# Product-key experts: 52 activation rows and 32 gate rows kept, one-hots by pairs of tokens, another spill layout

## The chip, the cores and the metric

The kernel runs on one core of one Trainium2 chip. The metric is the device time of one launch in microseconds. The core has TensorE (PE in the rows; PEld is its weight load), VectorE (DVE), ScalarE (ACT), GpSimd (POOL) and SyncE (SP, which here only issues DMAs), and 16 DMA engines.

## The reference, cut to what matters

The network has two blocks over 256 tokens of width 1024 (272 with the meta tokens in the first). The change lies in the last layer, a product-key mixture of 128 x 128 single-neuron experts:

```
q = (tok @ w_q)                                  # 8 heads x 2 halves x 128
s = einsum('nhpc,hpkc->nhpk', q, sub_keys)       # 128 scores per half
s_top, i_top = top_k(s, 16)                      # 16 keys of each half
best, pos = top_k(s_top[0] + s_top[1], 16)       # 16 pairs per head: 128 experts a token
gate = softmax(best)
act = gelu(u_emb[expert] . tok) * gate
out = sum over the 128 experts of act * v_emb[expert]
```

The kernel does not gather rows of u_emb and v_emb. It computes gelu(u . tok) for all 16384 experts, multiplies by a dense gate that is zero outside the selected experts, and multiplies by all of v_emb.

## The kernel before, in words

All matrix products are split into a high and a low part (three fp32r products each: L311, L312, L313). A weight tile of 128x1024 comes by DMA into `st` (3 buffers), ScalarE writes its high half `wh` (L279), VectorE or GpSimd the low half `wl` (L280; `lo_engine` says which); `wh` and `wl` have 5 buffers each. Weights are taken in a fixed order: 16 tiles of `wq`, then the `pu` tiles (rows of u_emb, one tile of 128 experts for each value of the first key), then `pv` tiles (v_emb).

An expert block k is a pair: `ublock(k)` (24 products of 128x256 into `pu`, then gelu) and `vblock(k)` (12 products of 128x512 into four accumulators `peo`). Between them `gated` multiplies by the gate row k and splits (`bh`, `bl`).

The layer has a front and a tail. In the front the first N1 = 39 ublocks are computed and their activations kept in `H`, while the experts are being selected: `top16` and `select` work on VectorE (L1538 to L1591), then `gates()` builds the dense gate. For 4 tokens at a time `onehot` makes `gO` (one-hot of both keys, [128, 2, 128, 4], tokens innermost; L1703) and `gW` (the first one-hot times the high and the low part of the gate; L1705), both fp16; `product` multiplies the second key's one-hot (stationary) with the two weighted ones, 2 products of 128x128 per token (`pG`, L1715 and L1716), and ScalarE puts columns 0 to 38 into `G1` (kept, L1718) and the other 89 into a staging tile `gst` of 32 tokens (L1719), which goes out to `peGd` in device memory in four DMAs (L1741). How much of this stands between two ublocks is set by a budget: each ublock adds GB = 3.0 (GB2 = 5.0 in the gate stage), each step of the generator takes off a figure that stands for its time:

```
due += self.GB2 if self.grp else self.GB
while gen is not None and due > 0:
    step = next(gen, None)
    ...
```

The list scheduler of the framework then orders the instructions of each engine by its own costs; each engine issues its own list strictly in order.

Behind the front, 39 vblocks use `H` and `G1`; then in the tail ublock(k + 1) and vblock(k) alternate for the other 89, with gate rows read back from `peGd` two at a time (`gl`, L1808). In the front the low halves of `wq` and `pu` are made by GpSimd, all later ones by VectorE.

Of the kernel before, what the change touches and what calls it, by code (L numbers as in the profile page):

```python
# [21 lines left out]
P = 128  # L22
# [15 lines left out]
# ---------------------------------------------------------------- host layout  # L38
# [17 lines left out]
def prep(i):  # L56
# [34 lines left out]
    # second block  # L91
# [32 lines left out]
def shape_consts():  # L124
    """Masks and selectors that depend on shapes alone."""
    a = {}
    p = np.arange(P)
    hd, ix = p // 64, p % 64
    same = hd[:, None] == hd[None, :]
    m = np.arange(64)[None, :]  # L130
    lt = (ix[:, None] < m).astype(np.float32)
    a["k_mask"] = np.ascontiguousarray(np.stack([lt, ix[:, None] <= m, -lt], axis=1).astype(np.float32))
    t, u = ix[:, None], ix[None, :]
    lv = []
    for b in (16, 32):
# [21 lines left out]
class Null:  # L157
    """Takes any call; used to walk the program once for the order in which it uses its weights."""
# [20 lines left out]
# ---------------------------------------------------------------- kernel  # L179
class Kern:  # L180
# [50 lines left out]
    # ---- weight stream  # L231
# [17 lines left out]
    def lo_engine(self, key, k):  # L249
        if key[0] == "wq" or (key[0] == "pu" and key[1] < self.N1):  # L250
            return self.nc.gpsimd
        if key[0] in ("w_rw", "w_ml", "w_gt") and k % self.PM == 0:
            return self.nc.gpsimd
        return self.nc.vector
# [60 lines left out]
    # ---- rms statistics  # L315
# [64 lines left out]
    def post(self, fg, ssq, h, T, name):  # L380
        """h += fg * rstd; returns the per-chunk updater."""
# [11 lines left out]
    # ---- FFN  # L393
# [55 lines left out]
    # ---- neighbourhood attention  # L449
# [13 lines left out]
    def na(self, xh, xl, R, gpost):  # L463
# [12 lines left out]
        nc.gpsimd.dma_start(bq, io["na_bqkv"])  # L476
        nc.vector.tensor_scalar_mul(bq[:, 0:8], bq[:, 0:8], 0.125)
        bo = ap.tile([P, C], F32, name="na_bo")
        nc.gpsimd.dma_start(bo, io["na_bo"])
# [199 lines left out]
    # ---- differential attention  # L679
    def da(self, xh, xl, R, gpost):  # L680
# [12 lines left out]
        nc.gpsimd.dma_start(sg, io["da_sg"])  # L693
        nc.vector.tensor_scalar_mul(sg, sg, 1.0 - LAMBDA_INIT)
        lp = ap.tile([P, 4, 64], F32, name="da_lp")
        nc.gpsimd.dma_start(lp.rearrange("p a b -> p (a b)"), io["da_lam"].to_broadcast([P, 256]))
# [187 lines left out]
    # ---- second block: mixers  # L884
# [10 lines left out]
    def mixers(self, h, xh, xl, R):  # L895
# [103 lines left out]
        def head_in(hh, S):  # L999
            """projections of a head: q, k with their convolution, v, output gate"""  # L1000
# [31 lines left out]
        def head_mid(hh, S):  # L1032
            """scores, their product with the values, mean and variance"""
# [48 lines left out]
        def heads_out():  # L1082
            """norm of all heads and output gate"""
# [23 lines left out]
        def filler():  # L1107
            """half a projection at a time, each followed by a step of what is due"""
# [36 lines left out]
        # ------------------------------------------------ RWKV  # L1145
# [129 lines left out]
        # [chunk, c, row, column] of 128 x 128 with 128 words between: diagonal blocks lie at one stride  # L1275
# [49 lines left out]
        def solve():  # L1325
            """inverse of the 128 unit triangular 16 x 16 blocks on the diagonals"""
# [145 lines left out]
        # ------------------------------------------------ merge, output  # L1472
# [52 lines left out]
    # ---- product-key experts  # L1525
    N1 = 39
# [4 lines left out]
    GB2 = 5.0  # L1531
# [12 lines left out]
    def select(self, tp, scr, b, v, ix, out):  # L1544
        """from the best 16 keys of each half to the 128 experts of a token; yields the time of each step"""
# [48 lines left out]
    def peer(self, h):  # L1594
        nc, io = self.nc, self.io
        T, N1 = NT, self.N1
        N2 = P - N1
# [9 lines left out]
        iota4 = ap.tile([P, P, 4], F16, name="iota4")  # L1607
        nc.vector.tensor_copy(iota4, self.iota.unsqueeze(2).to_broadcast([P, P, 4]))
# [30 lines left out]
        H = ap.tile([P, N1, T], F32, name="peH")  # L1639
        G1 = ap.tile([P, N1, T], F32, name="peG1")  # L1640
        gd = dp.tile([P, N2, T], F32, name="peGd")

        # ---- queries, scores, the best 16 keys of each half
# [25 lines left out]
        def gates():  # L1669
# [25 lines left out]
            # gate of every expert and token, G[i2, i1, t]  # L1695
            SG = self.SG
            sh = [P, 2, P, 4]
            gs_ = gst_.enter_context(self.tc.tile_pool(name="pegs", bufs=2))
            with self.tc.tile_pool(name="peg", bufs=2) as gp:
                def onehot(t1):  # L1700
                    tb = slice(t1, t1 + 4)
                    OB, W = (gp.tile(sh, F16, tag=f"g{n}", name=f"g{n}_{t1}") for n in "OW")
                    nc.vector.tensor_tensor(OB, iota4[:, None].to_broadcast(sh),  # L1703
                                            iT[:, :, None, tb].to_broadcast(sh), op=ALU.is_equal)
                    nc.vector.tensor_mul(W, OB[:, 0:1].to_broadcast(sh), gT[:, :, None, tb].to_broadcast(sh))  # L1705
                    return t1, OB, W

                def product(t1, OB, W):
# [4 lines left out]
                    p = self.acc(f"pG_{t1}").rearrange("p (t e) -> p t e", t=4)  # L1713
# [3 lines left out]
                    pe = p.rearrange("p t e -> p e t")  # L1717
                    nc.scalar.mul(G1[:, :, t1:t1 + 4], pe[:, 0:N1], 1.0 / self.GS)  # L1718
                    nc.scalar.mul(st[:, :, t1 - t0:t1 - t0 + 4], pe[:, N1:], 1.0 / self.GS)  # L1719
                    if t1 + 4 == t0 + SG:  # L1720
                        spills.extend((t0, st, slice(N2 * q // 4, N2 * (q + 1) // 4)) for q in range(4))
                    if t1 // 4 % 2:
                        spill()
# [3 lines left out]
                for t1 in range(0, T, 4):  # L1727
                    wait.append(onehot(t1))
                    if len(wait) > 1:
                        product(*wait.pop(0))  # L1730
                    yield 1.3
# [20 lines left out]
        for k in range(N1):  # L1752
# [28 lines left out]
        def gated(k, a, g):  # L1781
            ah = a2.tile([P, T], F32R, tag="bh", name=f"bh_{k}", bufs=3)
            al = a2.tile([P, T], F32R, tag="bl", name=f"bl_{k}", bufs=3)
            i = nc.vector.tensor_mul(a, a, g)
            j, _ = self.split(a, ah, al)
            if k < N1:
# [7 lines left out]
        for k in range(N1):  # L1794
# [8 lines left out]

        def ub(k):
            if (k - N1) % 2 == 0:
                n = min(2, P - k)
                g = vp.tile([P, 2, T], F32, tag="gl", name=f"gl_{k}", bufs=3)
                nc.sync.dma_start(g[:, :n], gd[:, k - N1:k - N1 + n])  # L1808
                hb["g"] = g
            a = vp.tile([P, T], F32, tag="ha", name=f"ha_{k}")  # L1810
            ublock(k, a)
            hb[k] = gated(k, a, hb["g"][:, (k - N1) % 2])

        fg = H[:, 0:4].rearrange("p k t -> p (k t)")
        ub(N1)
        for k in range(N1, P - self.FIN):
            if k == N1 + 8:
# [31 lines left out]
    # ---- whole  # L1849
# [54 lines left out]
```

## Time and profile before

| what | value |
|---|---|
| median of 3 runs | 2359.03 us (2357.69 to 2366.51) |
| span of the profiled execution | 2363.3 us; the page gives no other time of it, so the span stands for its time |
| TensorE busy in it | 2258.3 us, 96% |
| mean granted clock | 0.976 |
| front: first ublock to first output product | 1528.5 to 1746.2 us |
| 39 vblocks from kept rows | 1746.2 to about 1856 us |
| tail, 89 pairs | about 1856 us to the end |

A busy TensorE is not a TensorE at its peak, since its products are pipelined: how far apart two products start says more than how long one lasts. "issue" in a view is time in which an engine waited for nothing that the profile shows.

### The profile page before, as it was taken

The numbers are of one execution on the slowest core, as the hardware profiler recorded it, in microseconds if no ns is written. First come the engines' busy times: TensorE is split into PE (matmuls) and PEld (weight loads), VectorE is DVE, ScalarE is ACT, GpSimd is POOL, SyncE is SP. The second block draws the span as 40 slices with busy tenths as digits, with TensorE's granted clock in tenths as the row PEclk, the third lists the DMA queues.
The fourth block names the chain that finished last, engine by engine and source line by source line (L and its number), as shares of the span: only waits on it lengthen the run. The fifth ranks groups of instructions, "written<-read, shape, count | busy, mean of one in ns | idle before, by whom it ended". The sixth has DMA issues, their size and how long they took to land. (4 is left out here: it accounts for less than half of the span.)

```text
span 2363.3 us, 42332 instructions
## 1 busy us (share of the span) xinstructions
PE 2258.3 (96%) x16616; PEld 2148.1 (91%) x16616; DVE 1570.7 (66%) x2834; ACT 1170.8 (50%) x1992; POOL 380.8 (16%) x335
## 2 busy tenths in 40 slices
PE   8999999999999999999878999987999999999998
PEld 8999989999999889999878998986888899999997
DVE  6656777664765677765689647897777555555555
ACT  6444655443544456554544544544455444444444
POOL 1101211110210121210361112773200000000000
PEclk9999999999999999999989999997999999999999
DMA  6555433555455443555434325444896566666664
GB/s 207 178 169 160 149 109 115 183 170 176 153 178 173 140 142 102 182 183 182 141 105 126 119 68 184 161 152 97 144 203 227 200 210 209 210 214 209 210 209 144
DMA packets 217143, 389.56 MB, mean 165 GB/s; under 512 B 110272, under 2 KB 120272, under 8 KB 216816
## 3 DMA queue, kind: packets, MB, share of 16 engines
q1 hardware_dynamic: 216800, 386.71, 53.1%
q8 instruction: 131, 2.15, 0.4%
q14 instruction: 68, 0.56, 0.1%
q0 software_dynamic: 144, 0.15, 0.0%
HBM read 371.87 MB, written 14.94 MB: 164 GB/s over the span
## 5 line engine op out<-in xcount | busy, mean ns | idle before, releaser
L279 ACT ACTIVATE wh<-st 128x1024 fp32r<-128x1024 f32 (+2 forms) x680 | 703.8, 1037 | 789.1 <-PE peo L1773 146.9
L280 DVE TENSOR_TENSOR wl<-st,wh 128x1024 fp32r<-128x1024 f32 (+2 forms) x610 | 750.4, 1231 | 488.2 <-ACT wh L279 486.4
L311 PE MATMUL pg_ffn<-xh_n,wh 128*128 128x272 f32 (+1 forms) x1408 | 406.6, 291 | 12.7 <-ACT wh L279 8.1
L313 PE MATMUL pg_ffn<-xh_n,wl 128*128 128x272 f32 (+1 forms) x1408 | 408.1, 291 | 0.4 <-DVE wl L280 0.4
L312 PE MATMUL pg_ffn<-xl_n,wh 128*128 128x272 f32 (+1 forms) x1408 | 407.7, 290 | 0.0
L311 PE MATMUL pu<-xh_pe,wh 128*128 128x256 f32 x1024 | 292.5, 286 | 0.8 <-ACT peH L1748 0.8
L313 PE MATMUL pu<-xh_pe,wl 128*128 128x256 f32 x1024 | 291.2, 284 | 0.0
L312 PE MATMUL pu<-xl_pe,wh 128*128 128x256 f32 x1024 | 291.1, 284 | 0.0
L311 PEld LDWEIGHTS pg_ffn<-xh_n,wh 128*128 128x128 f32 x1408 | 268.4, 192 | 13.1 <-ACT wh L279 8.1
L313 PEld LDWEIGHTS pg_ffn<-xh_n,wl 128*128 128x128 f32 x1408 | 269.6, 192 | 0.8 <-DVE wl L280 0.8
L312 PEld LDWEIGHTS pg_ffn<-xl_n,wh 128*128 128x128 f32 x1408 | 270.1, 192 | 0.1
L280 POOL TENSOR_TENSOR wl<-st,wh 128x1024 fp32r<-128x1024 f32 x70 | 172.1, 2471 | 257.4 <-ACT wh L279 236.5
L1773 PE MATMUL peo<-wh,bh 128*128 128x512 f32 x512 | 203.0, 399 | 1.1 <-ACT bh L459 1.1
L1773 PE MATMUL peo<-wh,bl 128*128 128x512 f32 x512 | 202.1, 395 | 0.0
L311 PE MATMUL pd_ffn<-mh_ffn,wh 128*128 128x272 f32 (+1 forms) x704 | 201.9, 287 | 0.0
L1773 PE MATMUL peo<-wl,bh 128*128 128x512 f32 x512 | 201.4, 393 | 0.0
L312 PE MATMUL pd_ffn<-ml_ffn,wh 128*128 128x272 f32 (+1 forms) x704 | 201.4, 286 | 0.0
L313 PE MATMUL pd_ffn<-mh_ffn,wl 128*128 128x272 f32 (+1 forms) x704 | 201.3, 286 | 0.0
L311 PEld LDWEIGHTS pu<-xh_pe,wh 128*128 128x128 f32 x1024 | 196.1, 192 | 5.1 <-ACT peH L1748 1.0
L312 PEld LDWEIGHTS pu<-xl_pe,wh 128*128 128x128 f32 x1024 | 196.7, 192 | 3.6
L313 PEld LDWEIGHTS pu<-xh_pe,wl 128*128 128x128 f32 x1024 | 196.7, 192 | 0.1
L409 POOL TENSOR_TENSOR t_ffn<-t_ffn,t_ffn 128x272 f32<-128x272 f32 (+1 forms) x88 | 73.6, 838 | 455.3 <-DVE t_ffn L408 390.4
(626 smaller groups left out, 4747.4 us busy)
## 6 DMA issues: line engine op xcount, KB each, us to landing
st<-wgu SPq DMA_DIRECT2D x176, 512.0 KB, 3.5
st<-pu SPq DMA_DIRECT2D x128, 512.0 KB, 3.3
st<-pv SPq DMA_DIRECT2D x128, 512.0 KB, 3.4
st<-wd SPq DMA_DIRECT2D x64, 448.0 KB, 3.3
st<-wd SPq DMA_DIRECT2D x32, 512.0 KB, 3.4
st<-na_qkv SPq DMA_DIRECT2D x24, 512.0 KB, 3.4
st<-da_qkv SPq DMA_DIRECT2D x24, 512.0 KB, 3.7
gl<-peGd SPq DMA_DIRECT2D x44, 256.0 KB, 3.7
```

Source lines behind the costliest of these rows:

```text
L279: i1 = nc.scalar.activation(hi[:, :w], s[:, :w], AF.Copy)
L280: i2 = self.lo_engine(plan[k], k).tensor_sub(lo[:, :w], s[:, :w], hi[:, :w].bitcast(F32))
L311: mm(out, wh, xh, start=start, stop=False, **kw)
L312: mm(out, wh, xl, start=False, stop=False, **kw)
L313: mm(out, wl, xh, start=False, stop=stop, **kw)
L409: nc.gpsimd.tensor_mul(t2[:, :T], t1[:, :T], t2[:, :T])
L1773: mm(po[2 * b + j], x_[:, b * P:(b + 1) * P], w_[:, 4 * j:4 * j + 4].rearrange("p k m -> p (k m)"), start=k == 0 and n == 0, stop=k == P - ...
```

## The change

1. `H` keeps 52 rows in place of 39 (NH), `G1` keeps 32 in place of 39 (NG); gate rows 32 to 127 (96 in place of 89) go through device memory. So 13 ublocks move from the tail into the front, and vblocks 32 to 51 read their gate rows back.
2. One step of the gate stage is 8 tokens in place of 4: four VectorE instructions of 128x1024 (O1, W0, W1, O2), each of shape [4, 128, 2], two tokens innermost. TensorE reads the one-hots at a step of 2 fp16 elements in place of 4. O1 has one buffer, the others two.
3. The budget is taken off after each of the four instructions (0.7), and GB2 is 2.1.
4. `peGd` is laid out by blocks of 32 tokens, so that a spill writes runs of 3 KB per partition in place of 128 bytes, and a read-back reads runs of 256 bytes in place of 2 KB.
5. GpSimd makes the low halves of `pu` only up to k = 30 (NP); VectorE makes them from 31 on.
6. Four small loads of the attention stages go from GpSimd's queue to SyncE's, and the scratch of the software DMA queue is cut to 2048 bytes.

```diff
-        if key[0] == "wq" or (key[0] == "pu" and key[1] < self.N1):
+        if key[0] == "wq" or (key[0] == "pu" and key[1] < self.NP):
...
-        nc.gpsimd.dma_start(bq, io["na_bqkv"])
+        nc.sync.dma_start(bq, io["na_bqkv"])
...
-    N1 = 39
+    NH = 52
+    NG = 32
+    NP = 31
...
-    GB2 = 5.0
+    GB2 = 2.1
...
-        H = ap.tile([P, N1, T], F32, name="peH")
-        G1 = ap.tile([P, N1, T], F32, name="peG1")
-        gd = dp.tile([P, N2, T], F32, name="peGd")
+        H = ap.tile([P, NH, T], F32, name="peH")
+        G1 = ap.tile([P, NG, T], F32, name="peG1")
+        gd = dp.tile([T // SG, P, N2, SG], F32, name="peGd")
...
-                def onehot(t1):
-                    tb = slice(t1, t1 + 4)
-                    OB, W = (gp.tile(sh, F16, tag=f"g{n}", name=f"g{n}_{t1}") for n in "OW")
-                    nc.vector.tensor_tensor(OB, iota4[:, None].to_broadcast(sh),
-                                            iT[:, :, None, tb].to_broadcast(sh), op=ALU.is_equal)
-                    nc.vector.tensor_mul(W, OB[:, 0:1].to_broadcast(sh), gT[:, :, None, tb].to_broadcast(sh))
-                    return t1, OB, W
+                def pairs(x, t1):
+                    return x[:, t1:t1 + 8].rearrange("p (q s) -> p q s", s=2).unsqueeze(2).to_broadcast(sh)
+                def onehot(t1):
+                    O1, O2, W0, W1 = (gp.tile(sh, F16, tag=f"g{n}", name=f"g{n}_{t1}", bufs=1 if n == "O1" else 2)
+                                      for n in ("O1", "O2", "W0", "W1"))
+                    nc.vector.tensor_tensor(O1, iota2[:, None].to_broadcast(sh), pairs(iT[:, 0], t1), op=ALU.is_equal)
+                    yield 0.7
+                    nc.vector.tensor_mul(W0, O1, pairs(gT[:, 0], t1))
+                    yield 0.7
+                    nc.vector.tensor_mul(W1, O1, pairs(gT[:, 1], t1))
+                    yield 0.7
+                    nc.vector.tensor_tensor(O2, iota2[:, None].to_broadcast(sh), pairs(iT[:, 1], t1), op=ALU.is_equal)
+                    wait.append((t1, O2, W0, W1))
+                    yield 0.7
...
-                    for q in range(4):
-                        mm(p[:, q], OB[:, 1, :, q], W[:, 0, :, q], start=True, stop=False)
-                        mm(p[:, q], OB[:, 1, :, q], W[:, 1, :, q], start=False, stop=True)
+                    for u in range(0, 8, 4):
+                        p = self.acc(f"pG_{t1}_{u}").rearrange("p (t e) -> p t e", t=4)
+                        for q in range(4):
+                            a, b = divmod(u + q, 2)
+                            mm(p[:, q], O2[:, a, :, b], W0[:, a, :, b], start=True, stop=False)
+                            mm(p[:, q], O2[:, a, :, b], W1[:, a, :, b], start=False, stop=True)
...
-                nc.sync.dma_start(gd[:, q, t0:t0 + self.SG], st[:, q])
+                nc.sync.dma_start(gd[t0, :, q], st[:, q])
...
-        for k in range(N1):
+        for k in range(NH):
             ublock(k, H[:, k])
...
-        for k in range(N1):
+        for k in range(NG):
             vblock(k, *gated(k, H[:, k], G1[:, k]))
...
+        def spilled(k):
+            if (k - NG) % 2 == 0:
+                n = min(2, P - k)
+                g = vp.tile([P, T // SG, 2, SG], F32, tag="gl", name=f"gl_{k}", bufs=3)
+                nc.sync.dma_start(g[:, :, :n], gd[:, :, k - NG:k - NG + n].rearrange("u p k t -> p u k t"))
+                hb["g"] = g
+            return hb["g"][:, :, (k - NG) % 2]
...
+        for k in range(NG, NH):
+            vblock(k, *gated(k, H[:, k], spilled(k)))
...
-    nc = bacc.Bacc("TRN2", target_bir_lowering=False, num_devices=1)
+    nc = bacc.Bacc("TRN2", target_bir_lowering=False, num_devices=1, dynamic_dma_scratch_size=2048)
```

TensorE's list up to the gate stage is the same in both kernels. The next rows are TensorE's at the end of the front of the kernel before; `pu_20648` is the last of the 39 ublocks, each `pG` piece 8 products of 4 tokens, `peo` the first output products.

```order
L1716 MATMUL pG_20555<-gW_20536,gO_20535 128x128
L311 MATMUL pu_20603<-xh_pe,wh_20332 128x256
...
L311 MATMUL pu_20648<-xh_pe,wh_20410 128x256
...
L1715 MATMUL pG_20570<-gW_20552,gO_20551 128x128
...
L1715 MATMUL pG_20586<-gW_20567,gO_20566 128x128
...
L1715 MATMUL pG_20629<-gW_20583,gO_20582 128x128
...
L312 MATMUL pu_20648<-xl_pe,wh_20410 128x256
...
L1773 MATMUL peo_20674<-wh_20505,bh_20678 128x512
```

The same place in the changed kernel; `pu_20765` is the last of the 52 ublocks, and the number behind gW and gO is a step's first token.

```order
L311 MATMUL pu_20703<-xh_pe,wh_20539 128x256
...
L1728 MATMUL pG_0_20730<-gW_168_20596,gO_168_20595 128x128
...
L311 MATMUL pu_20765<-xh_pe,wh_20601 128x256
...
L1728 MATMUL pG_0_20793<-gW_176_20692,gO_176_20691 128x128
...
L1728 MATMUL pG_0_20824<-gW_184_20755,gO_184_20754 128x128
...
L1728 MATMUL pG_0_20856<-gW_192_20818,gO_192_20817 128x128
...
L1728 MATMUL pG_0_21066<-gW_248_21037,gO_248_21036 128x128
...
L1785 MATMUL peo_21090<-wh_20636,bh_21094 128x512
```

Before, the last gate products stand inside the last ublock. Now 22 of the 32 steps stand between ublocks 22 and 51 (three steps to four ublocks, each step's 16 products in one piece), and the steps of tokens 176 to 255, ten of them, stand behind the last ublock with nothing between them.

VectorE's list in the middle of the gate stage of the kernel before, with the low halves on GpSimd's own list:

```order
L1703 TENSOR_TENSOR gO_20362<-iota_17358,pei 128x1024
L1703 TENSOR_TENSOR gO_20377<-iota_17358,pei 128x1024
L1705 TENSOR_TENSOR gW_20363<-gO_20362,peg 128x1024
L1705 TENSOR_TENSOR gW_20378<-gO_20377,peg 128x1024
L1703 TENSOR_TENSOR gO_20393<-iota_17358,pei 128x1024
```

And of the changed kernel, where the low halves stand on VectorE's list from ublock 31 on:

```order
L280 TENSOR_TENSOR wl_20540<-st_20413,wh_20539 128x1024
L1711 TENSOR_TENSOR gW_152_20470<-gO_152_20468,peg 128x1024
L1713 TENSOR_TENSOR gW_152_20471<-gO_152_20468,peg 128x1024
L1715 TENSOR_TENSOR gO_152_20469<-iota_17358,pei 128x1024
L1709 TENSOR_TENSOR gO_160_20531<-iota_17358,pei 128x1024
L280 TENSOR_TENSOR wl_20602<-st_20475,wh_20601 128x1024
```

Per 8 tokens both lists hold four instructions of 128x1024; what is new on VectorE's list is the low halves between them.

## Rows read from the trace of the kernel before

**Rows 1.** Page: busy time of each engine; granted clock in 40 slices.

```profile
PE 2258.3 (96%) x16616; PEld 2148.1 (91%) x16616; DVE 1570.7 (66%) x2834; ACT 1170.8 (50%) x1992; POOL 380.8 (16%) x335
...
PEclk9999999999999999999989999997999999999999
```

**Rows 2.** Stretches from A to B: length, busy per engine, clock, DMA share, GB/s.

```profile
1530.00:1584.00 54.00, 53.23 (x446) 52.70 (x446) 53.44 (x164) 32.16 (x40) 47.10 (x20) 1.00 0.51 172
1584.00:1600.00 16.00, 4.50 (x36) 4.33 (x35) 15.03 (x32) 2.43 (x5) 0.15 (x1) 0.75 0.12 41
1600.00:1612.00 12.00, 5.17 (x36) 5.08 (x35) 12.00 (x12) 4.56 (x7) 9.87 (x4) 0.78 0.38 133
1612.00:1746.00 134.00, 118.96 (x938) 114.18 (x935) 102.78 (x129) 62.42 (x162) 33.65 (x13) 0.93 0.78 136
...
1860.00:2340.00 480.00, 480.00 (x3073) 433.53 (x3073) 266.91 (x343) 228.95 (x342) 0.00 (x0) 1.00 0.63 210
```

**Rows 3.** Waits, 1600 to 1746 us: waiting, waited for, total, times, longest.

```profile
DVE gO L1703 <- PE pG L1716: 30.4, 50, 2.4
PE pG L1715 <- DVE gW L1705: 21.0, 13, 6.8
```

**Rows 4.** Timeline of VectorE and GpSimd in the gate stage: start, length, instruction.

```profile
1608.72 2.84 DVE L1705 TENSOR_TENSOR gW<-gO,peg 128x1024 f16<-128x1024 f16 x1
...
1611.69 0.68 DVE L1705 TENSOR_TENSOR gW<-gO,peg 128x1024 f16<-128x1024 f16 x1
...
1653.49 2.39 POOL L280 TENSOR_TENSOR wl<-st,wh 128x1024 fp32r<-128x1024 f32 x1 [6.47 <-ACT wh L279]
1654.63 2.41 DVE L1703 TENSOR_TENSOR gO<-iota,pei 128x1024 f16<-128x1024 f16 x2 [1.80 <-PE pG L1716]
1656.96 1.28 DVE L1705 TENSOR_TENSOR gW<-gO,peg 128x1024 f16<-128x1024 f16 x2
```

**Rows 5.** Tile gO: ns min/median/max, first and last start.

```profile
L1716 PE MATMUL pG<-gW,gO x256: 293/298/303, 1611.7 to 1744.6; 128*128 128x128 f16 x128
L1703 DVE TENSOR_TENSOR gO<-iota,pei x64: 678/693/2851, 1600.6 to 1741.9; 128x1024 f16<-128x1024 f16 x64
L1705 DVE TENSOR_TENSOR gW<-gO,peg x64: 676/684/2842, 1608.7 to 1742.7; 128x1024 f16<-128x1024 f16 x64
```

**Rows 6.** Groups by line, 1612 to 1746 us: busy us, mean ns.

```profile
L280 DVE TENSOR_TENSOR wl<-st,wh 128x1024 fp32r<-128x1024 f32 x2 | 2.4, 1224 | 0.2 <-ACT wh L279 0.2
```

**Rows 7.** Timeline of TensorE, gate and block products: start, length.

```profile
1613.19 0.30 PE L1716 MATMUL pG<-gW,gO 128*128 128x128 f16 x1
...
1613.90 0.30 PE L1716 MATMUL pG<-gW,gO 128*128 128x128 f16 x1
...
1614.52 0.41 PE L311 MATMUL pu<-xh_pe,wh 128*128 128x256 f32 x1
1614.73 0.41 PE L312 MATMUL pu<-xl_pe,wh 128*128 128x256 f32 x1
...
1616.98 0.30 PE L1716 MATMUL pG<-gW,gO 128*128 128x128 f16 x1
...
1618.15 0.30 PE L1716 MATMUL pG<-gW,gO 128*128 128x128 f16 x1
```

**Rows 8.** Chain of waits: start, length; end of front, and two tail pairs.

```profile
1746.18 109.47 PE peo L1773 x468
...
1990.98 2.80 PE peo L1773 x12
...
1996.61 2.80 PE peo L1773 x12
```

**Rows 9.** DMA, 1620 to 1760 us: packets; queue's packets, MB, share of 16 engines.

```profile
DMA packets 88516, 20.76 MB, mean 148 GB/s; under 512 B 86144, under 2 KB 86144, under 8 KB 88504
...
q1 hardware_dynamic: 88504, 20.60, 82.7%
```

**Rows 10.** DMA, 1860 to 2300 us: the same.

```profile
DMA packets 28167, 92.63 MB, mean 211 GB/s; under 512 B 3136, under 2 KB 3136, under 8 KB 28135
...
q1 hardware_dynamic: 28135, 92.18, 62.9%
```

More of the change, by code (lines that the diff above doesn't have):

```diff
@@ L475, in na @@
         bq = ap.tile([P, 24], F32, name="na_bq")
-        nc.gpsimd.dma_start(bq, io["na_bqkv"])
+        nc.sync.dma_start(bq, io["na_bqkv"])
         nc.vector.tensor_scalar_mul(bq[:, 0:8], bq[:, 0:8], 0.125)
         bo = ap.tile([P, C], F32, name="na_bo")
-        nc.gpsimd.dma_start(bo, io["na_bo"])
+        nc.sync.dma_start(bo, io["na_bo"])
         vph, vpl, qms = [], [], []
@@ L692, in da @@
         sg = ap.tile([P, 1], F32, name="da_sg")
-        nc.gpsimd.dma_start(sg, io["da_sg"])
+        nc.sync.dma_start(sg, io["da_sg"])
         nc.vector.tensor_scalar_mul(sg, sg, 1.0 - LAMBDA_INIT)
         lp = ap.tile([P, 4, 64], F32, name="da_lp")
-        nc.gpsimd.dma_start(lp.rearrange("p a b -> p (a b)"), io["da_lam"].to_broadcast([P, 256]))
+        nc.sync.dma_start(lp.rearrange("p a b -> p (a b)"), io["da_lam"].to_broadcast([P, 256]))
         lt = ap.tile([P, 2, 64], F32, name="da_lt")
@@ L1595, in peer @@
         nc, io = self.nc, self.io
-        T, N1 = NT, self.N1
-        N2 = P - N1
+        T, NH, NG = NT, self.NH, self.NG
+        N2 = P - NG
         mm = nc.tensor.matmul
@@ L1606, in peer @@
         nc.vector.tensor_copy(self.iota16, self.iota[:, 0:16].unsqueeze(2).to_broadcast([P, 16, 16]))
-        iota4 = ap.tile([P, P, 4], F16, name="iota4")
-        nc.vector.tensor_copy(iota4, self.iota.unsqueeze(2).to_broadcast([P, P, 4]))
+        iota2 = ap.tile([P, P, 2], F16, name="iota2")
+        nc.vector.tensor_copy(iota2, self.iota.unsqueeze(2).to_broadcast([P, P, 2]))
         ssq = self.new_ssq("pe")
@@ L1638, in peer @@
         iT = ap.tile([P, 2, T], F16, name="pei")
-        H = ap.tile([P, N1, T], F32, name="peH")
-        G1 = ap.tile([P, N1, T], F32, name="peG1")
-        gd = dp.tile([P, N2, T], F32, name="peGd")
+        H = ap.tile([P, NH, T], F32, name="peH")
+        G1 = ap.tile([P, NG, T], F32, name="peG1")
+        SG = self.SG
+        gd = dp.tile([T // SG, P, N2, SG], F32, name="peGd")
         ts_ = ExitStack()
@@ L1694, in gates, with product @@
             ts_.close()
-            SG = self.SG
-            sh = [P, 2, P, 4]
+            sh = [P, 4, P, 2]
             gs_ = gst_.enter_context(self.tc.tile_pool(name="pegs", bufs=2))
             with self.tc.tile_pool(name="peg", bufs=2) as gp:
+                def pairs(x, t1):
+                    return x[:, t1:t1 + 8].rearrange("p (q s) -> p q s", s=2).unsqueeze(2).to_broadcast(sh)
                 def onehot(t1):
-                    tb = slice(t1, t1 + 4)
-                    OB, W = (gp.tile(sh, F16, tag=f"g{n}", name=f"g{n}_{t1}") for n in "OW")
-                    nc.vector.tensor_tensor(OB, iota4[:, None].to_broadcast(sh),
-                                            iT[:, :, None, tb].to_broadcast(sh), op=ALU.is_equal)
-                    nc.vector.tensor_mul(W, OB[:, 0:1].to_broadcast(sh), gT[:, :, None, tb].to_broadcast(sh))
-                    return t1, OB, W
-                def product(t1, OB, W):
+                    O1, O2, W0, W1 = (gp.tile(sh, F16, tag=f"g{n}", name=f"g{n}_{t1}", bufs=1 if n == "O1" else 2)
[9 more added lines that the diff above has]
+                    yield 0.7
+                def product(t1, O2, W0, W1):
                     nonlocal st
@@ L1712, in product @@
                         st = gs_.tile([P, N2, SG], F32, tag="gst", name=f"gst_{t1}")
-                    p = self.acc(f"pG_{t1}").rearrange("p (t e) -> p t e", t=4)
-                    for q in range(4):
-                        mm(p[:, q], OB[:, 1, :, q], W[:, 0, :, q], start=True, stop=False)
-                        mm(p[:, q], OB[:, 1, :, q], W[:, 1, :, q], start=False, stop=True)
[L1717 to L1723, printed above, removed]
+                    for u in range(0, 8, 4):
[4 more added lines that the diff above has]
+                            mm(p[:, q], O2[:, a, :, b], W1[:, a, :, b], start=False, stop=True)
+                        pe = p.rearrange("p t e -> p e t")
+                        t2 = t1 + u
+                        nc.scalar.mul(G1[:, :, t2:t2 + 4], pe[:, 0:NG], 1.0 / self.GS)
+                        nc.scalar.mul(st[:, :, t2 - t0:t2 - t0 + 4], pe[:, NG:], 1.0 / self.GS)
+                    if t1 + 8 == t0 + SG:
+                        spills.extend((t0 // SG, st, slice(N2 * q // 4, N2 * (q + 1) // 4)) for q in range(4))
+                    spill()
                 st, wait = None, []
                 self.grp = True
-                for t1 in range(0, T, 4):
-                    wait.append(onehot(t1))
+                for t1 in range(0, T, 8):
+                    yield from onehot(t1)
                     if len(wait) > 1:
                         product(*wait.pop(0))
-                    yield 1.3
                 for x in wait:
@@ L1783, in gated @@
             al = a2.tile([P, T], F32R, tag="bl", name=f"bl_{k}", bufs=3)
-            i = nc.vector.tensor_mul(a, a, g)
+            if k < NG:
+                i = nc.vector.tensor_mul(a, a, g)
+            else:
+                a3 = a.rearrange("p (u t) -> p u t", t=SG)
+                i = nc.vector.tensor_mul(a3, a3, g)
             j, _ = self.split(a, ah, al)
-            if k < N1:
+            if k < NH:
                 for n in range(self.AH):
@@ L1802, in peer @@
         vp = vs.enter_context(self.tc.tile_pool(name="pev", bufs=2))
-        def ub(k):
[L1805 to L1809, printed above, removed]
+        def spilled(k):
[5 more added lines that the diff above has]
+            return hb["g"][:, :, (k - NG) % 2]
+        def ub(k):
+            g = spilled(k)
             a = vp.tile([P, T], F32, tag="ha", name=f"ha_{k}")
             ublock(k, a)
-            hb[k] = gated(k, a, hb["g"][:, (k - N1) % 2])
+            hb[k] = gated(k, a, g)
+        for k in range(NG, NH):
+            vblock(k, *gated(k, H[:, k], spilled(k)))
         fg = H[:, 0:4].rearrange("p k t -> p (k t)")
-        ub(N1)
-        for k in range(N1, P - self.FIN):
-            if k == N1 + 8:
+        ub(NH)
+        for k in range(NH, P - self.FIN):
+            if k == NH + 8:
                 nc.sync.dma_start(fg, io["fg"].to_broadcast([P, D]))
```

## The prediction

> **What bounds the kernel now.** I read the page first: TensorE is busy 96% of the span and the granted clock dips in few slices [rows 1], so a gain can only come from the places where TensorE waits or runs at half clock. The table of stretches shows where they are [rows 2]. The tail has no room: in 480 us TensorE is busy for 480 at clock 1.00, and the chain of waits goes over TensorE alone, one pair of blocks every 1996.61 - 1990.98 = 5.63 us, of which 2.80 are the output products [rows 8], so that a ublock costs 5.63 - 2.80 = 2.83 us there (24 products, 0.118 us apart). The front has room: 11.5 us idle in 1584 to 1600, 6.8 in the next 12 us, and in the gate stage, 1612 to 1746, 15 us idle beside a clock of 0.93 [rows 2].
>
> In the gate stage two engines lock each other. VectorE makes 128 one-hots of 0.685 us (medians 693 and 684 ns) [rows 5], 87.7 us, and GpSimd's low halves take 33.65 us [rows 2]. They do not overlap: while GpSimd ran from 1653.49 to 1655.88, two one-hots that started inside that time took 2.41 us in place of the 1.28 of the next two, and they ended 1.16 us after GpSimd [rows 4]. So 87.7 + 33.65 = 121 of 134 us are taken on these two together. With two buffers VectorE also waits for TensorE's gate products, 30.4 us in 50 waits, and TensorE for VectorE, 21.0 us in 13 waits, 6.8 at the longest [rows 3].
>
> **Part 1: up to the first gate product.** Both lists are the same to the middle of the first one-hots, so selection and its idle TensorE before 1600 stay. Before, the second weighted one-hot was ready at 1611.69 + 0.68 = 1612.4 [rows 4]; the change puts as many VectorE instructions ahead of its first complete step. TensorE has ublocks 20 to 22 to run from 1600 on, 3 x 2.83 = 8.5 us, a little more at half clock, and so waits some 2.5 us in place of 6.8. I start both sums at 1612.4.
>
> **Part 2: the gate products.** Two gate products start 0.117 us apart at full clock (1616.98 to 1618.15, ten steps). In a stretch of half clock, where block products are 1614.73 - 1614.52 = 0.21 apart in place of 0.118, gate products are still 0.118 apart (1613.19 to 1613.90, six steps) [rows 7]. So it is not TensorE's clock that sets them. A block product streams 256 columns in the same 0.118 us, a gate product only 128, but those are read at a step of four fp16 elements; the change halves that step. The cost afterwards lies between 0.059 us (half of a block product's 0.118, for half the columns) and 0.118 (as now); it can't rise, since only the step shrinks. I take 0.075, nearer to the block product, because a rate that ignores the clock and belongs to the only operands with a step points at the reading. A step of 8 tokens is then 16 x 0.075 = 1.20 us, and 1.89 at the upper end.
>
> [...]
>
> **Part 3: ublocks 23 to 30 with steps 0 to 5.** TensorE: 8 x 2.83 + 6 x 1.20 = 29.8 us. VectorE and GpSimd together: five low halves still on GpSimd at 2.39 [rows 4], 12.0; the one-hots of steps 1 to 7, 28 x 0.685 = 19.2; three low halves on VectorE at 1.224 [rows 6], 3.7; sum 34.9. The larger counts: 34.9.
>
> **Part 4: ublocks 31 to 51 with steps 6 to 21.** TensorE: 21 x 2.83 + 16 x 1.20 = 78.6. VectorE: 64 x 0.685 + 21 x 1.224 = 69.5, and GpSimd is out of it. So TensorE sets the time: 78.6, with VectorE's work beside it. [...]
>
> **Part 5: steps 22 to 31, behind the last ublock.** Here TensorE has only 1.20 us per step and VectorE needs 4 x 0.685 = 2.74. After ublock 51 VectorE makes one low half (its buffer is freed by that block), 1.2, and the last three instructions of step 24, 2.05; then seven more steps, 7 x 2.74 = 19.2; TensorE's last step 1.2: 23.7 us. From the last gate product to the first output product it was 1746.18 - 1744.6 = 1.6 us [rows 5, 8], and that stays.
>
> **Part 6: the tail.** 13 ublocks fewer: 13 x 2.83 = 36.8 us less. VectorE's and ScalarE's work in it only shrinks.
>
> **Part 7: DMA.** In the tail 28135 packets took 62.9% of 16 x 440 us, 4428 us; without the 3136 small ones about 0.177 us each [rows 10]. In the gate stage 88504 packets took 82.7% of 16 x 140 = 1852 us; taking 2360 large ones at 0.177 off, 86144 of 128 bytes took 16.6 ns each [rows 9]. A read-back becomes 128 x 8 = 1024 packets of 256 bytes, by bounds of 16.6 ns (as 128 bytes) and 33 (twice that): 1.1 to 2.1 us of all sixteen engines per 11.26 us, in which 37% or 4.2 us are free. So it costs nothing as long as the loads are issued a few us ahead, which three buffers allow; the spills get lighter (2848 packets become 128 of 3 KB). [...] The four small loads land long before they are used and SyncE's list has them behind the same weight loads: nothing.
>
> **Sum.** First output product: 1612.4 + 34.9 + 78.6 + 23.7 + 1.6 = 1751.2, against 1746.2 now: +5.0. With the tail's -36.8: -31.8. I add 4 us of friction, an estimate: before, 7% of 134 us were missing from the clock, 9.4 us, in stretches that followed waits or long runs of gate products; of these I expect less than half. That makes -28. The profiled span is 2363.3, the median of the runs 2359.0, inside the runs' own spread; from the median I predict 2331.
>
> **Rivals.**
> B, gate products stay at 0.118 us. [...] Against: the indifference to the clock. Part 3 is still 34.9 (TensorE 34.0); part 4 is 21 x 2.83 + 16 x 1.89 = 89.7; the end 3.9 + 19.2 + 1.9 = 25.0. First output at 1763.6, +17.4, with tail and friction -15.4: 2344.
>
> [...]
>
> D, nothing measurable: the change does what it says, but step 31 is late or weights are not there, since SyncE's list has twelve spills in one piece behind the last steps and the weight loads of vblock 8 and later stand behind them; ten microseconds of TensorE waiting, beside B's sum, leave -5: 2354. Against: eight tiles of pv, 22 us of work, are loaded ahead of these spills.
>
> **How the numbers follow.** The change forecast, A, has a chance of 0.48, with a range of its own of 2322 to 2339 (0.059 us would give part 4 another 4 us, with friction gone another 4); B 0.30; C 0.12; D 0.10. A measurement of this kernel tells 0.5%, 12 us, from no change. Faster: all of A, 0.24 of B and a little of D, 0.73; within 0.5%: the rest of B and most of D, 0.14; slower: C, 0.13 with D's worst. The range reaches over A, B and D, 2316 to 2360, and leaves C out.
>
> **What would show it.** In the changed profile: gate products 0.06 to 0.09 us apart (A) or 0.118 (B); four one-hots of about 0.69 us per step (against C: 1.2); first output product near 1755; the ten last steps with VectorE busy without a gap and TensorE waiting about 1.5 us before each; 76 tail pairs still 5.63 us apart; read-backs that nobody waits for. I am wrong if the front's end moves past 1775, or if a tail pair takes longer than 5.7 us.

## The result, and the profile after

The changed kernel takes 2327.32 us (median of 4 runs, 2324.7 to 2333.81) where the kernel before takes 2362.77 (4 runs on the same chip): ratio 0.9843, 95% interval 0.9824 to 0.9863. The forecast was 2331, range 2316 to 2360. The profiled execution, with a span of 2332.0 us, is the slowest of the four; before's span was 2363.3, so the two traces differ by 31.3 us where the medians differ by 35.

The page of the changed kernel, in answer to [rows 1]: TensorE lost 28 us of busy time, GpSimd 23, VectorE 1.5.

```profile
PE 2230.2 (96%) x16616; PEld 2120.9 (91%) x16616; DVE 1569.2 (67%) x2842; ACT 1165.8 (50%) x1992; POOL 357.8 (15%) x323
...
PEclk9999999999999999999998999898989999999999
```

The stretches of the changed kernel, with the columns of [rows 2]:

```profile
1584.00:1600.00 16.00, 4.26 (x30) 4.09 (x29) 15.03 (x34) 3.45 (x7) 0.27 (x1) 0.72 0.09 33
1600.00:1612.00 12.00, 8.95 (x70) 8.75 (x69) 12.00 (x8) 5.70 (x9) 11.87 (x5) 0.93 0.48 151
...
1640.00:1726.00 86.00, 84.61 (x862) 83.64 (x860) 73.38 (x98) 52.54 (x124) 0.00 (x0) 1.00 0.70 234
1726.00:1752.00 26.00, 17.17 (x135) 13.82 (x136) 21.22 (x38) 11.51 (x36) 0.00 (x0) 0.60 0.49 186
...
1748.90:1840.00 91.10, 91.10 (x379) 73.14 (x380) 59.06 (x97) 42.56 (x64) 0.00 (x0) 0.97 0.62 204
```

From 1640 to 1722 TensorE has ublocks and gate products with almost no gap at full clock, GpSimd is out, and VectorE keeps up with time to spare. What is lost now lies at both ends: 6.9 us of waiting before the first gate product, hardly changed, and the 26 us behind the last ublock (1722.60 to 1748.88), most of them at the lower clock (0.60 in 1726 to 1752). The waits of 1600 to 1752 us say the same, in answer to [rows 3] (there 21.0 and 30.4 us):

```profile
PE pG L1728 <- DVE gO L1715: 9.1, 2, 6.9
PE pG L1728 <- DVE gW L1711: 5.4, 5, 1.4
...
DVE gO L1715 <- PE pG L1729: 1.3, 3, 0.5
```

TensorE's gate products, against [rows 7]: the first two rows lie at half clock (granted 0.50 in 1615.80 to 1617.50; TensorE has just waited for 6.9 us, and the block products behind them stand 0.21 us apart), fourteen products apart (1617.39 - 1615.90 over 14 is 0.106 us); the other two at full clock (1.00 in 1632.80 to 1633.80), fifteen apart (1633.73 - 1632.86 over 15 is 0.058 us). Before, they were 0.117 to 0.118 us apart at either clock (0.50 in 1613.10 to 1614.00, 1.00 in 1616.90 to 1618.30).

```profile
1615.90 0.31 PE L1729 MATMUL pG<-gW,gO 128*128 128x128 f16 x1
...
1617.39 0.31 PE L1729 MATMUL pG<-gW,gO 128*128 128x128 f16 x1
...
1632.86 0.23 PE L1728 MATMUL pG<-gW,gO 128*128 128x128 f16 x1
...
1633.73 0.22 PE L1729 MATMUL pG<-gW,gO 128*128 128x128 f16 x1
```

The one-hots keep their length [rows 5], with the columns of that view (the maxima are those beside GpSimd):

```profile
L1709 DVE TENSOR_TENSOR gO<-iota,pei x32: 675/682/2914, 1599.6 to 1743.9; 128x1024 f16<-128x1024 f16 x32
L1713 DVE TENSOR_TENSOR gW<-gO,peg x32: 675/683/2901, 1607.8 to 1745.2; 128x1024 f16<-128x1024 f16 x32
```

In the tail two pairs are still 2004.74 - 1999.12 = 5.62 us apart [rows 8], and TensorE waits for nothing there:

```profile
1999.12 2.80 PE peo L1785 x12
...
2004.74 2.80 PE peo L1785 x12
```

Three more rows of TensorE give the borders of the table below: the start of ublock 31, of the first step behind the last ublock, and the last gate product.

```profile
1648.08 0.36 PE L311 MATMUL pu<-xh_pe,wh 128*128 128x256 f32 x1
...
1722.60 0.23 PE L1728 MATMUL pG<-gW,gO 128*128 128x128 f16 x1
...
1747.31 0.31 PE L1729 MATMUL pG<-gW,gO 128*128 128x128 f16 x1
```

The prediction's steps beside what the trace shows:

| step | predicted | measured |
|---|---|---|
| 1: first whole step of one-hots ready | 1612.4 | 1615.75 |
| 2: gate products apart, full clock | 0.075 us | 0.058 us |
| 3: ublocks 23 to 30 and their steps | 34.9 | 32.3 (to 1648.1) |
| 4: ublocks 31 to 51 and their steps | 78.6 | 74.5 (to 1722.6) |
| 5: steps behind the last ublock | 23.7 | 24.7 (to 1747.3) |
| first output product | 1751.2 | 1748.9 |
| friction | 4 | 2.7 at the tail's start; more inside steps 3 and 5 |
| tail | -36.8 | -33.9, with the 2.7 in it |

### The profile page after: what moved, and what is told of

Same layout as the page of the kernel before. It is cut to its first block, busy times and chain, and to the rows that moved or that the text cites. A ratio compares the mean times of both kernels' runs of the same rounds, so it can differ in the third digit from the quotient of the medians.

```text
span 2332.0 us, 42185 instructions
## 1 busy us (share of the span) xinstructions
PE 2230.2 (96%) x16616; PEld 2120.9 (91%) x16616; DVE 1569.2 (67%) x2842; ACT 1165.8 (50%) x1992; POOL 357.8 (15%) x323
## 5 line engine op out<-in xcount | busy, mean ns | idle before, releaser
L280 DVE TENSOR_TENSOR wl<-st,wh 128x1024 fp32r<-128x1024 f32 (+2 forms) x618 | 760.1, 1231 | 490.8 <-ACT wh L279 488.8
L280 POOL TENSOR_TENSOR wl<-st,wh 128x1024 fp32r<-128x1024 f32 x62 | 151.9, 2465 | 183.5 <-ACT wh L279 169.1
```

What stands on the lines that cost most here:

```text
L280: i2 = self.lo_engine(plan[k], k).tensor_sub(lo[:, :w], s[:, :w], hi[:, :w].bitcast(F32))
```

## The experiments

Theory: the change turned a gate stage held by VectorE and GpSimd into one held by TensorE, whose gate products became twice as fast by their reading step (0.117 us apart before, 0.058 after, at full clock); the 13 rows are worth what their ublocks cover. Rivals: the faster products alone are the gain; or the spill layout is.

The layer itself begins up to 7.7 us apart in the profiled executions, so a front is measured from its first product (`pwq`) to the first output product. These are the two rows for the changed kernel, 1748.9 - 1472.2 = 276.7 us:

```profile
L311 PE MATMUL pwq<-xh_pe,wh x128: 277/280/579, 1472.2 to 1526.6; 128*128 128x256 f32 x128
...
L1785 PE MATMUL peo<-wh,bh x512: 392/399/796, 1748.9 to 2324.6; 128*128 128x512 f32 x171
```

| kernel | ratio to the kernel before (95%) | front |
|---|---|---|
| before | 1 | 271.9 |
| changed | 0.9843 (0.9824 to 0.9863) | 276.7 |
| e1 moving operand at four | 0.9924 (0.9903 to 0.9944) | 295.2 |
| e2 stationary operand at four | 0.9860 (0.9839 to 0.9882) | 275.3 |
| e3 pairs alone, 39 rows | 0.9953 (0.9929 to 0.9976) | 258.1 |
| e4 front low halves on GpSimd | 0.9884 (0.9863 to 0.9905) | 285.2 |
| e5 budget 2.8 | 0.9794 (0.9776 to 0.9811) | 265.3 |
| e6 low halves from 22 on VectorE | 0.9816 (0.9797 to 0.9834) | 267.0 |
| e7 39 activation rows | 0.9929 (0.9909 to 0.9948) | 256.4 |
| e8 old spill layout | 0.9890 (0.9871 to 0.9910) | 280.3 |
| e9 = e5 + e6 | 0.9769 (0.9752 to 0.9787) | 254.1 |
| e10 = e9, budget 3.2 | 0.9755 (0.9735 to 0.9775) | 251.9 |
| e11 = e9, from 16 on VectorE | 0.9736 (0.9717 to 0.9754) | 246.2 |
| e12 = e11, budget 3.2 | 0.9729 (0.9704 to 0.9753) | 245.4 |

e3 and e7 keep 39 rows and have 13 more ublocks in the tail, 34 us; the other fronts compare directly. A difference of 0.001 is 2.4 us, and two ratios of different chips are uncertain by about 0.0028 against each other (two half-widths of 0.002).

**e1 and e2: which operand's step.** The shapes are given in short; in e1 the one-hots of both weighted parts change, in e2 the stationary one alone.

```diff
 e1:
-  O1, W0, W1: [P, 4, P, 2]
+  O1, W0, W1: [P, 2, P, 4]
-  mm(p[:, q], O2[:, a, :, b], W0[:, a, :, b], ...)
+  mm(p[:, q], O2[:, a, :, b], W0[:, u // 4, :, q], ...)
 e2:
-  O2: [P, 4, P, 2]
+  O2: [P, 2, P, 4]
-  mm(p[:, q], O2[:, a, :, b], W0[:, a, :, b], ...)
+  mm(p[:, q], O2[:, u // 4, :, q], W0[:, a, :, b], ...)
```

> The changed kernel (2327.3 us) with the weighted one-hots W0, W1 (the moving operand of the gate products) and O1 at four tokens innermost again; O2, the stationary operand, stays at two. Theory: the reading step of the MOVING operand sets the pitch. Then gate products are 0.118 us apart again in place of 0.058; 22 steps of 16 products stand between ublocks where TensorE never waits, 22 x 16 x 0.06 = 21 us later: about 2348 us, and VectorE's instructions still about 0.68 us long. Rival: the stationary operand's step sets it: pitch 0.058, 2327 us.

> The changed kernel (2327.3 us) with O2, the stationary operand of the gate products (the weight load), at four tokens innermost, O1, W0, W1 at two. Theory (moving operand sets the pitch): pitch stays 0.058, weight loads perhaps longer than 0.097 us, 2327 us. Rival (the weight load's reading step sets the pitch, and what stands between two products): 0.118, about 2348 us.

Gate products of e1, twelve steps between the rows, 0.117 us each; then of e2, fourteen steps, 0.059 each:

```profile
1647.74 0.30 PE L1735 MATMUL pG<-gW,gO 128*128 128x128 f16 x1
...
1649.14 0.29 PE L1735 MATMUL pG<-gW,gO 128*128 128x128 f16 x1
```

```profile
1648.72 0.22 PE L1736 MATMUL pG<-gW,gO 128*128 128x128 f16 x1
...
1649.55 0.22 PE L1736 MATMUL pG<-gW,gO 128*128 128x128 f16 x1
```

e1 is 0.0081, 19 us, above the changed kernel, its front 18.5 longer; e2 is within the uncertainty. The moving operand's step sets the pitch. In e2 the weight load takes 113 ns against 97 in the changed kernel, which the pitch does not show; whether the stationary operand's step is the reason is not shown, since in e1, where that step is unchanged, the loads beside the slower products take 115 to 118. VectorE's instructions stay at 0.68 us in all of them.

**e3: pairs alone.**

```diff
 against the changed kernel:
-    NH = 52; NG = 32; NP = 31; GB2 = 2.1
+    NH = 39; NG = 39; NP = 39; GB2 = 5.4
-  gd = dp.tile([T // SG, P, N2, SG], ...)
+  gd = dp.tile([P, N2, T], ...)
```

> Only the one-hots by pairs, in a frame of the kernel before: 39 rows kept of both, all front low halves on GpSimd, the old spill layout, and a budget of 5.4 in the gate stage, which gives the pace of before (7.7 instructions of 128x1024 per ublock). Theory: gate products 0.058 us apart free 512 x 0.06 = 30 us of TensorE, but the stage is held by VectorE and GpSimd, which exclude each other (128 x 0.60 + 13 x 2.5 = 110 us of the 134): most of the 30 us turns into waiting for one-hots, the front ends some 5 to 15 us earlier: about 2352 us (2345 to 2360) against 2362.8 before. Rival: the shorter products are the gain by themselves: 2335 us.

0.9953: 11 us faster than before, not 28. (e3 also keeps the finer budget and the moved small loads, so even the 11 need not be the pairs' alone.) TensorE's products are faster (920 in 92.77 us of its gate stage, 0.101 each, gate and block products together, where before it was 938 in 118.96, 0.127 [rows 2]), yet it has 92.77 of 119 us to do there, beside 109.21 of VectorE, the time that it was held back by GpSimd included, and 33.85 of GpSimd:

```profile
1612.00:1731.00 119.00, 92.77 (x920) 88.61 (x920) 109.21 (x130) 58.33 (x160) 33.85 (x13) 0.88 0.88 153
```

From 1600 to 1760 us it waits 28 us for one-hots (the view of waits):

```profile
PE pG L1728 <- DVE gW L1711: 15.3, 8, 2.9
PE pG L1728 <- DVE gO L1715: 8.6, 4, 7.6
PE pG L1729 <- DVE gW L1713: 4.4, 9, 1.6
```

**e4: low halves back on GpSimd** (`NP = 52` in place of 31).

> The changed kernel (2327.3 us) with the low halves of all 52 front ublocks on GpSimd (31 to 51 no longer on VectorE). Theory: GpSimd's 2.4 us and VectorE's one-hots exclude each other, so beside ublocks 31 to 51 the two need 64 x 0.60 + 21 x 2.45 = 90 us where TensorE needs 76 to 79: some 12 us later, TensorE waits for one-hots between ublocks: about 2339 us (2335 to 2347). Rival: low halves on GpSimd are beside everything, no difference: 2327 us.

0.9884, 10 us slower than the changed kernel, front 8.5 longer. Nineteen low halves on GpSimd fill VectorE to 84.38 of 86 us:

```profile
1640.00:1726.00 86.00, 78.28 (x773) 76.01 (x773) 84.38 (x71) 47.33 (x108) 46.90 (x19) 1.00 0.60 209
```

Among the waits from 1600 to 1752 us, TensorE now waits twelve times for O2, not twice:

```profile
PE pG L1728 <- DVE gO L1715: 17.1, 12, 7.0
```

**e5: a faster budget** (`GB2 = 2.8` in place of 2.1).

> The changed kernel (2327.3 us) with a budget of 2.8 in place of 2.1: four VectorE instructions, one whole step, per ublock; three steps stand behind the last ublock in place of ten. In the changed kernel these ten took 20.6 us where TensorE needs 0.92 each. Theory: what is left to gain is the uncovered steps; VectorE needs 4 x 0.60 + 1.15 = 3.55 us per ublock where TensorE needs 2.92 + 0.92 = 3.84, so it keeps up; seven steps x (2.06 - 0.92) = 8 us, and less half clock behind: about 2317 us. Rival: VectorE falls behind beside the ublocks (GpSimd is still on up to ublock 30), so the waiting only moves: 2327 us.

0.9794, 12 us faster than the changed kernel, front 11.4 shorter. VectorE carries one step per ublock in time, and with three steps behind the last ublock the stretch from there to the first output product is 7.41 us long in place of 26.28 (first a stretch beside the ublocks in e5, then this one in e5, then the same in the changed kernel):

```profile
1640.00:1726.00 86.00, 86.00 (x901) 85.03 (x899) 82.69 (x116) 55.26 (x138) 0.00 (x0) 1.00 0.68 239
...
1727.33:1734.74 7.41, 3.90 (x50) 3.46 (x49) 4.92 (x9) 5.30 (x16) 0.00 (x0) 0.79 0.66 225
```

```profile
1722.60:1748.88 26.28, 16.07 (x162) 13.16 (x160) 22.57 (x37) 14.21 (x44) 0.00 (x0) 0.66 0.42 157
```

**e6: no backlog on GpSimd** (`NP = 22`).

> The changed kernel (2327.3 us) with the low halves of ublocks 22 to 30 on VectorE in place of GpSimd. In the changed kernel GpSimd ran six of them back to back from 1600.1 to 1615.2 us while VectorE's first seven gate instructions took 2.4 to 2.9 us each in place of 0.3 to 0.7, and TensorE stood 6.9 us before the first gate product. Theory: the two engines exclude each other, so the step that failed in the prediction (first product at 1612.4, measured 1615.8) is this backlog: six low halves of 1.15 on VectorE cost 6.9 us in place of 15.1; first gate product some 4 to 6 us earlier, about 2322 us (2319 to 2325). Rival: the low halves come first on VectorE's list and delay the one-hots as much, or the selection before 1600 gets longer: 2327 or above.

In the changed kernel the six low halves and some of VectorE's instructions beside them are these (start, length):

```profile
1600.13 15.08 POOL L280 TENSOR_TENSOR wl<-st,wh 128x1024 fp32r<-128x1024 f32 x6 [15.86 <-ACT wh L279]
...
1602.63 2.88 DVE L1711 TENSOR_TENSOR gW<-gO,peg 128x1024 f16<-128x1024 f16 x1
...
1607.78 2.87 DVE L1713 TENSOR_TENSOR gW<-gO,peg 128x1024 f16<-128x1024 f16 x1
...
1610.58 2.44 DVE L1694 TENSOR_TENSOR peg<-pgr,peg 128x128 f16<-128x128 f32 x1
1612.93 2.82 DVE L1715 TENSOR_TENSOR gO<-iota,pei 128x1024 f16<-128x1024 f16 x1
1615.68 0.68 DVE L1709 TENSOR_TENSOR gO<-iota,pei 128x1024 f16<-128x1024 f16 x1
```

In e6 the same instructions take their own 0.68 us with low halves of 1.21 between them, and TensorE is busy for all of 1600 to 1612 (the stretch, then the timeline):

```profile
1600.00:1612.00 12.00, 12.00 (x114) 11.91 (x113) 12.00 (x24) 5.45 (x11) 0.00 (x0) 0.95 0.56 180
```

```profile
1601.53 0.68 DVE L1711 TENSOR_TENSOR gW<-gO,peg 128x1024 f16<-128x1024 f16 x1
...
1603.60 0.68 DVE L1715 TENSOR_TENSOR gO<-iota,pei 128x1024 f16<-128x1024 f16 x1
1604.20 1.21 DVE L280 TENSOR_TENSOR wl<-st,wh 128x1024 fp32r<-128x1024 f32 x1
```

The first gate product comes 136.4 us after the layer's first product in place of 143.6, the front is 9.7 shorter. The ratio, 0.0027 lower, is at the edge of what these runs can tell. e9 and e5 differ by the same edit, by 0.0025 and 11.2 us of front; the two pairs together bear it out.

**e7: 39 activation rows** (`NH = 39`).

> The changed kernel (2327.3 us) with 39 activation rows kept in place of 52 (32 gate rows as in the changed kernel). Theory: the 13 more ublocks are worth what they cover. Without them 20 steps in place of 10 stand behind the last ublock, each 2.06 us where TensorE needs 0.92: 10 x 1.14 = 11 us more waiting, and more half clock: about 2339 us (2336 to 2345). Rival: the rows bring nothing, only the faster products do: 2327 us.

0.9929, by the ratios 20 us slower than the changed kernel, more than the 11 expected; in the profiled executions its front is 20.3 us shorter and the tail 34.0 longer, 13.7 net. The steps were priced too low: 2.06 us for each uncovered one, but the ten of the changed kernel took 24.7, not 20.6, and the twenty of e7 take 53.5 (1670.09 to 1723.61), so that ten more cost 28.8, 2.9 each. They run at a lower clock, 0.60 over the last 35 us of the gate stage:

```profile
1689.00:1724.00 35.00, 23.19 (x200) 18.65 (x197) 29.56 (x47) 16.29 (x51) 0.00 (x0) 0.60 0.35 136
```

**e8: the old spill layout.**

```diff
-  gd = dp.tile([T // SG, P, N2, SG], ...)
+  gd = dp.tile([P, N2, T], ...)
-  nc.sync.dma_start(gd[t0, :, q], st[:, q])
+  nc.sync.dma_start(gd[:, q, t0 * SG:t0 * SG + SG], st[:, q])
...
```

The read-backs follow the old layout too.

> The changed kernel (2327.3 us) with the spill layout of the kernel before (128-byte runs out, 2 KB runs back). Theory: nothing on the path; the DMA share of the gate stage goes back from 0.6 to about 0.8, weights still come in time: 2327 us within 4. Rival: the small packets delayed the weight loads, and the new layout is a good part of the gain: TensorE waits for weights in the gate stage, 2340 us or more.

My theory fell here, and the rival is right in kind: 0.9890, by the ratios 11 us (4 to 18) slower than the changed kernel; the front of the one profiled execution is 3.6 longer, and where the rest lies is not shown. The DMA queue of 1620 to 1760 us is full:

```profile
q1 hardware_dynamic: 96816, 27.00, 98.3%
```

ScalarE waits for weights in the gate stage (the view of waits):

```profile
ACT wh L279 <- DMA st<-pu: 25.7, 8, 6.6
```

At one place it waits 5.70 us; VectorE's low half stands behind it and the one-hots behind that, so that TensorE waits 5.41 us (the timeline of both). In all, TensorE waits 19.3 us for one-hots in 1600 to 1760, 15.4 in the changed kernel, which is about the 3.6 of the front:

```profile
1728.85 1.06 ACT L279 ACTIVATE wh<-st 128x1024 fp32r<-128x1024 f32 x1 [5.70 <-DMA st<-pv]
...
1733.02 0.29 PE L1728 MATMUL pG<-gW,gO 128*128 128x128 f16 x1 [5.41 <-DVE gO L1715]
```

The changed kernel's queue in the same 140 us, in answer to [rows 9]:

```profile
q1 hardware_dynamic: 9918, 28.57, 59.6%
```

And the same wait in it:

```profile
ACT wh L279 <- DMA st<-pu: 6.3, 3, 3.8
```

**e9 to e12: a better version.** Only `NP` and `GB2` differ from the changed kernel: e9 22 and 2.8, e10 22 and 3.2, e11 16 and 2.8, e12 16 and 3.2.

> Both of e5 and e6 in one kernel: low halves from ublock 22 on by VectorE, budget 2.8. Theory: e6 brings the first gate product forward by some 6 us (counted from the end of selection: 17.8 us in the changed kernel, 11.7 in e6) and TensorE then never waits beside the ublocks; e5 takes off the uncovered steps. The two are at different places, so they add: about 2311 us, 0.977 of the kernel before (e5 0.979, e6 0.982, changed kernel 0.984). Rival: VectorE, with all low halves and one step per ublock from 22 on (3.55 of 3.84 us), becomes the bound, and the start won is lost again: 0.979 or above.

> As e9 with a budget of 3.2: 4.6 VectorE instructions per ublock, no step behind the last ublock. VectorE needs 4.6 x 0.60 + 1.15 = 3.9 us per ublock, TensorE 2.92 + 1.14 x 0.92 = 3.97: no margin is left. Theory (covered steps are free): 3 x 1.1 = 3 us faster than e9. Rival (the margin is gone: VectorE's low halves come late, and TensorE waits for weights beside the ublocks): same as e9 or slower.

> As e9 with the low halves from ublock 16 on by VectorE: six more leave GpSimd. In the changed kernel GpSimd's last six low halves before the gate stage (1567.6 to 1584.3 us) fall on seven VectorE instructions of the selection that take 10.8 us longer than their like without them (3.42 for 1.21, 2.10 for 0.2), while its max and find instructions beside earlier low halves keep their 0.41 us. Theory: the exclusion holds here too; six low halves of 1.15 on VectorE cost 6.9 in place of 10.8, selection ends some 4 us earlier, and TensorE's 11.7 us of waiting for it shrinks: 2 to 4 us faster than e9. Rival: VectorE is the bound of selection and every low half given to it makes it longer: 3 to 7 us slower than e9.

> e11 with the budget of e10 (3.2): low halves from ublock 16 on by VectorE, no step behind the last ublock. Theory: e10 was 0.0014 of the kernel before (3 us) below e9, because the last three steps found cover; the same three stand uncovered in e11, so 2299 us, 0.972 of the kernel before. Rival: VectorE, which has 3.9 of 3.97 us per ublock to do, now also starts earlier with low halves and falls behind: 0.9736 as e11, or slower.

e9 is 0.0074, 18 us, below the changed kernel: e5 and e6 add. e11 is another 0.0033 below e9 on the same chip, its front 7.9 us shorter, more than the 2 to 4 expected. Counted from the layer's first product, selection hands over its results 3 to 6 us earlier (TensorE's transposes at 119.5 to 121.9 us, in e9 from 125.2 on), and the 12.2 us that TensorE waits for them in e9 are gone: it is busy for 15.98 us of 1584 to 1600, in place of 4.26 in the changed kernel. What the ublocks that now run beside selection add to that was not taken apart.

```profile
1584.00:1600.00 16.00, 15.98 (x131) 15.44 (x131) 14.94 (x33) 12.11 (x16) 0.00 (x0) 1.00 0.48 166
```

One wait for a low half of VectorE takes part of their place:

```profile
PE pu L313 <- DVE wl L280: 3.9, 1, 3.9
```

The budget of 3.2 gave 3 us over e9 and 2 over e11, inside the uncertainty. e12, 2297.55 us, is the best version: 0.9729 (0.9704 to 0.9753) of the kernel before.

## Why the prediction was right, and where it was not

The change forecast, A, was the right case. Its decisive step, that a rate which ignores TensorE's clock belongs to an operand with a step, is shown by e1 and e2 (0.117 us with the moving operand at four, 0.059 with the stationary one at four); the pitch fell to the lower end of its bounds, 0.058 us, and follows the clock now (0.106 at half clock). Part 4 was 4.1 us shorter than summed: it had fifteen steps of 16 x 0.058 = 0.93 in place of sixteen of 1.20, which is 5.2 less (the sixteenth had gone into part 3), and its 21 ublocks took 2.88 each in place of 2.83, 1.1 more.

Rival B fell with it: the gate products did not stay at 0.118 us, and e1, with the moving operand at a step of four again, has them 0.117 apart again. The slower case, C, did not come about. No run shows the 1.2 us given for its one-hots, my estimate after the fp32 instruction of the same 1024 elements [rows 6]: runs of two still take 0.68 us, and follow each other every 0.60, so that VectorE had more slack beside the ublocks than the 69.5 of 78.6 us summed (63.97 of 75.10 in 1647.50 to 1722.60). Rival D did not come about: from 1748 to 1900 TensorE waits once, 1.3 us, and not for weights.

Part 1 failed. It counted as many VectorE instructions as before ahead of the first step, 1612.4, but not what GpSimd does beside them: six low halves, 15.1 us in one piece, as soon as TensorE starts again and frees buffers. The exclusion that the section on the bound showed in [rows 4] had to be applied there too. Before, this piece was four low halves, 9.87 us ([rows 2], 1600 to 1612), done by 1611.0, and the last two VectorE instructions ahead of 1612.4 ran undisturbed, in 0.28 and 0.68 us; now they fall beside the fifth and the sixth low half and take 2.44 and 2.82, 4.3 more, of which an earlier start gives back 1.0. TensorE runs three ublocks before its wait (8.95 us busy in 1600 to 1612, 5.17 before), which fits the two more buffers that come free; that this is the reason was not tried by itself. TensorE waited 6.9 us, no less than before, in place of 2.5; e6 takes the backlog away and the wait with it.

Part 3 was right for a wrong reason. Since those six low halves were done by 1615.2, VectorE and GpSimd had less than 34.9 us left; TensorE set the time: 8 x 2.83 + 7 x 0.93 = 29.2, and about 3 us of lower clock behind the wait (0.63 in 1616 to 1624, 8 x 0.37 = 3.0), 32.2. Parts 1 and 3 together were off by 0.75 us.

Part 5 came out within 1 us. VectorE's 0.60 per instruction would have made it shorter, but TensorE fell to half clock (0.50 in 1730 to 1740, 0.66 in the whole stretch), where a step of sixteen products, 0.106 us apart, takes 1.7 us, and VectorE waited for it three times, 1.3 us.

Part 7 priced the layout at nothing, and beside the kernel before that holds: the gate's read-backs make nobody late, as before (they land in 4.2 us, median; the queue's share in 1860 to 2300 us is 68.1% where [rows 10] has 62.9). But it missed that the old layout would no longer do: at the new pace it fills the queue (98.3% in e8). The lighter spills carry 11 us of the gain (4 to 18).

The tail's 36.8 us arrived as 33.9, since its first 91 us ran at clock 0.97: 91 x 0.03 = 2.7 us, behind the waits of the uncovered steps. Fewer of these do not take it away: in e5, with three, the first 91 us of the tail (1734.74 to 1825.84) still run at 0.98.

The friction of 4 us was argued otherwise and came out near by luck. It supposed that the clock missing in the gate stage would fall from 7% to less than half of that; in 1612 to 1746 us the clock was 0.91, where it had been 0.93. Much of this stands where TensorE waits for one-hots anyway; the part that counted, about 3 us behind the first wait, went into part 3, where there was room for it in the 34.9.

The parts are worth more undone than done: taking back the step, the low halves, the rows or the layout alone costs 19, 10, 20 and 11 us, 60 in all, of a gain of 37 by the same ratios; the pairs alone gave 11. So the parts do not add: each needs the others to find cover. The finer budget, the 32 gate rows in place of 39, the moved small loads and the smaller DMA scratch were not tried by themselves.

## What to carry to other kernels

Look at the distance between products at both clocks: a pitch that stayed the same at half clock (0.118 us) went here with the step of the moving operand (e1), and the layout of that operand is the place to look. Where two engines exclude each other, as GpSimd's low halves and VectorE's one-hots did here (2.8 to 2.9 us beside them in place of 0.68), apply it to every stretch in which both have work, the bursts after a long wait above all; a low half at half the price on the busier engine (1.21 us in place of 2.4) can be the cheaper one. When a stage gets faster, price again what was hidden beside it: the DMA share, and the steps that now stand without cover.

## What the runs showed of the hardware that was not expected

- The moving operand's step in fp16 elements sets the pitch of the 128-column gate products: 0.117 us at four (e1), 0.058 at two and full clock (0.106 at half). The stationary operand's step does not: at four (e2) the pitch is 0.059.
- GpSimd's low halves do not hold back every VectorE instruction. In the changed kernel, max and find instructions of 128x256 take 0.40 to 0.41 us beside four low halves in a row, which themselves take 2.38 each; in e11, behind its last low half on GpSimd, they take 0.42 to 0.43. A shift, a cast and an fp16 product beside the next low halves take 2.10 in place of 0.21, 2.10 in place of 0.27 (the cast in e11, where it has none beside it), and 3.42 in place of 1.21 (two of them in the rows below).

```profile
1557.32 0.41 DVE L1544 FIND_INDEX8 tkp<-tkb,tkc 128x8 uint32<-128x256 f32 x1
...
1570.35 2.10 DVE L1572 TENSOR_SCALAR tkpab<-tkp 128x128 uint32<-128x128 uint32 x1
...
1578.61 3.42 DVE L1581 TENSOR_TENSOR peG<-peG 128x2048 f16<-128x2048 f16 x1
```
